# Two trunk layers on one core: a quarter of layer 1's modulation columns moved to TensorE in the fifth k phase

## The chip, the cores and the metric

The kernel runs on one core of a Trainium2 chip. The metric is device time in microseconds, median of several executions. Before the change it is 1356.29 us (three runs, 1355.13 to 1356.93).

## The reference

Two layers are applied to 384 tokens (128 context tokens and 256 latent tokens) of width 2048, all in fp32. Each layer makes three modulation vectors per group from a conditioning vector (`c_ctx` for the context tokens, `c` for the latent ones), mixes the tokens, and adds the gated result:

```python
m = silu(cond) @ w_mod + b_mod            # w_mod: 2048 x 6144; shift, scale, gate of 2048 columns each
h = rmsnorm(x) * (1 + scale) + shift
y = x + gate * mixer(h @ w_in) @ w_out
```

Layer 0's mixer is a gated linear recurrence (HGRN2) beside grouped attention; layer 1's is windowed attention with a sink. Layer 1's shift and scale columns, 4096 of them, are needed only when layer 0 is done, since layer 1's `h` is made from layer 0's output.

## The kernel before

All engines' work is laid down by one Python program; a framework then schedules it: it goes by the order of the program, prefers what is marked high priority, and lets an instruction that it takes to be ready pass one that it takes to be not ready. On the chip each engine works its list strictly in that order.

**Products.** A weight piece of 128x1024 fp32 numbers is loaded (`w_piece`, L365), split on ScalarE into a rounded part `whi` and on VectorE into a rest `wlo`, and multiplied on TensorE with the tokens' two parts `hh` and `hl`, three products for each pair. So each weight number costs one load, one ScalarE cast, one VectorE subtraction and three matmuls. Most pieces belong to a `group` of 512 output columns (L375); their raw tiles are the four buffers of the tag `raw`.

**The start.** Layer 0's input can't be modulated until layer 0's shift and scale columns are known, so the first six groups of columns of `l0_w_in` are made in five phases of k tiles, `START = ((0, 1), (1, 3), (3, 6), (6, 10), (10, 16))` (L38): all six groups take the k tiles of a phase (`start_group`, L720, with raw tiles of their own, tag `sraw`, three buffers), and meanwhile TensorE makes the modulation columns of the next phase's k tiles (`start_mod`, L740). For that a `w_mod` block is the moving operand and the 32-column tile `cs32` of conditioning numbers the stationary one, so a matmul uses 32 of the array's 128 columns; k tiles 0, 1, 2, 3 modulo 4 go to four different strips of 32 (L751). A `start_mod` step loads one 512 KB block into a `raw` buffer and issues the matmuls of its k tiles: four of 256 columns in the usual form, eight of 128 in the other. fp32 matmuls stand in the trace as two records each. At the end of a pair the sums are copied out (`ev`), transposed, added up over the strips (`ms`), and biases are added (`mod_cols`, L249).

**Layer 1's modulation and all gates** are made on VectorE in the background. `mod_part(l, k0)` (L291) makes 1024 columns: 16 loads of 512 KB into `mraw` (three buffers, L271), for each of them two multiply-adds of 128x1024 into `acc`, then four matmuls with a matrix of ones, a copy, four transposes and `mod_cols`. The parts are a list, `mods` (L776): four parts for layer 1 (shift and scale columns), then the first gates of layer 0 (`mod_gates`, L311). `pump` (L348) is called after each piece of products. It may run a unit (one load and two multiply-adds) when two budgets allow it: `pace[1]` units per call, and a planner's clock, by which VectorE's planned work may not run ahead of TensorE's. Both clocks are added up from the program's own cost formulas (L56 to L66). In the start the pace is `RATE0 = 0.6` (L777), in the later groups 2.0.

The loop of the phases (L780) spreads the next phase's `start_mod` steps evenly over the steps of products; in the fifth phase there is nothing left to spread, and only products and `mods` units run:

```python
        for j, _ in enumerate(start_products(k0, k1)):
            while done < (j + 1) * n_nxt // n:
                next(nxt, None)
                done += 1
            pump()
```

After the fifth phase come the other groups of layer 0 (the first ones, 512 columns as moving operand, use the `raw` buffers again), the recurrence and the attention as queued side work, the output projection, and layer 1.

Of the kernel before, what the change touches and what calls it, by code (L numbers as in the profile page):

```python
# [7 lines left out]
F32 = mybir.dt.float32  # L8
# [3 lines left out]
ALU = mybir.AluOpType  # L12
AX = mybir.AxisListType

P = 128
D = 2048
KT = D // P
# [5 lines left out]
RATE0 = 0.6  # L23
RAWB = 4
HIB = 3
LOB = 2
T2B = 2
# [18 lines left out]
def trunk_kernel(ctx: ExitStack, tc: tile.TileContext, I, O):  # L46
# [39 lines left out]
    nc = Core()  # L86
# [3 lines left out]
    wpool = ctx.enter_context(tc.tile_pool(name="wpool", bufs=1))  # L90
    hpool = ctx.enter_context(tc.tile_pool(name="hpool", bufs=1))
    tpool = ctx.enter_context(tc.tile_pool(name="tpool", bufs=1))
    mpool = ctx.enter_context(tc.tile_pool(name="mpool", bufs=1))

    st_ctx = ctx.enter_context(ExitStack())
    spool = st_ctx.enter_context(tc.tile_pool(name="spool", bufs=1))
# [5 lines left out]
    def nm(s):  # L102
        uid[0] += 1
        return f"{s}_{uid[0]}"

    def px():
        return psx.tile([P, 512], F32, tag="px", name=nm("px"))

    def t6(tag, dt=F32):
        return tpool.tile([P, 1536], dt, tag=f"t{tag}", name=nm(f"t{tag}"))  # L110
# [6 lines left out]
    queue, due, pace = [], [], [0.0, 0.0]  # L117
# [24 lines left out]
    ident = ct[:, C_ID:C_ID + P]  # L142
# [39 lines left out]
    cs32 = spool.tile([P, KT * 32], F32, name="cs32").rearrange("p (k c) -> p k c", k=KT)  # L182
# [63 lines left out]
    def w_view(w, k0, nk, c0, n=512):  # L246
        return w[k0 * P:(k0 + nk) * P, c0:c0 + n].rearrange("(k p) c -> p k c", p=P)

    def mod_cols(l, k0, nk, cp):  # L249

        like = (lambda a: a.rearrange("p (h b) c -> p h b c", h=2)) if len(cp.shape) == 4 else (lambda a: a)
        nc.vector.tensor_tensor(
            out=like(modc[l][:, k0:k0 + nk, :]), in0=cp,
            in1=like(bcol[l][:, k0:k0 + nk].unsqueeze(2).broadcast_to([P, nk, 2])), op=ALU.add)
        if KT <= k0 < 2 * KT:
            q = slice(k0 - KT, k0 - KT + nk)
            nc.vector.scalar_tensor_tensor(
                out=acol[l][:, q, :], in0=modc[l][:, k0:k0 + nk, :], scalar=1.0,
                in1=gcol[l][:, q].unsqueeze(2).broadcast_to([P, nk, 2]), op0=ALU.add, op1=ALU.mult)
# [31 lines left out]
    def mod_part(l, k0):  # L291

        acc = yield from mod_acc(l, k0 * P)
        ps = px()
        for j in range(4):
            nc.tensor.matmul(ps[32 * j:32 * j + 32, :], lhsT=ones[:, 0:32],
                             rhs=acc[:, j % 2, 512 * (j // 2):512 * (j // 2) + 512], start=True, stop=True)
        ev = mpool.tile([P, 512], F32, tag="t2", bufs=T2B, name=nm("ev"))
        with tc.high_priority(BOOST):
            nc.scalar.copy(ev, ps)  # L300
        for _ in range(EVY):
            yield
        cp = px()
        for b in range(4):
            nc.tensor.transpose(cp[:, b * P:b * P + P], ev[:, b * P:b * P + P], ident)
        mod_cols(l, k0, 8, cp.rearrange("p (b h c r) -> p h b c r", b=4, h=2, c=2)[:, :, :, :, 0])
        yield
# [3 lines left out]
    def mod_gates(l, g0, tags, ready):  # L311

        acc = yield from mod_acc(l, 2 * D + 512 * g0)
        while not ready[0]:
            yield
        for i in range(2):
            c0 = 2 * D + 512 * (g0 + i)
            gb = t6(tags[i])[:, 0:1024].rearrange("p (c n) -> p c n", c=2)
            for c in range(2):
                nc.gpsimd.dma_start(gb[:, c], I[f"l{l}_b_mod"][c0:c0 + 512].partition_broadcast(P))  # L320
            for c in range(2):
                ps = px()
                a = acc[:, c, 512 * i:512 * i + 512]
                hi = mpool.tile([P, 512], F32R, tag="t2", bufs=T2B, name=nm("ahi"))
                nc.scalar.copy(hi, a)
                lo = mpool.tile([P, 512], F32R, tag="t2", bufs=T2B, name=nm("alo"))
                nc.vector.tensor_tensor(out=lo, in0=a, in1=hi.bitcast(F32), op=ALU.subtract)
                nc.tensor.matmul(ps, lhsT=ones_r, rhs=hi, start=True, stop=False)
                nc.tensor.matmul(ps, lhsT=ones_r, rhs=lo, start=False, stop=True)
                nc.vector.tensor_tensor(out=gb[:, c], in0=ps, in1=gb[:, c], op=ALU.add)  # L330
            gates[l, g0 + i] = gb
        yield
# [3 lines left out]
    mods, rows, now = [], [], []  # L336
# [123 lines left out]
    def modulate(l, q, xt, rb, hq=None, parts=((0, 4),)):  # L460

        hh, hl = hq_tiles(q) if hq is None else hq
        for k0, k1 in parts:
            x = xt[:, k0:k1]
            nc.vector.tensor_tensor(out=x, in0=x, in1=rb.unsqueeze(1).broadcast_to([P, k1 - k0, T]), op=ALU.mult)
            for k in range(k0, k1):
                for c, s in CT:
                    kt = 4 * q + k
                    nc.scalar.activation(xt[:, k, s], xt[:, k, s], AF.Identity, bias=modc[l][:, kt, c:c + 1],  # L469
                                         scale=acol[l][:, kt, c:c + 1])  # L470
            nc.scalar.copy(hh[:, k0:k1], x)  # L471
            nc.vector.tensor_tensor(out=hl[:, k0:k1], in0=x, in1=hh[:, k0:k1].bitcast(F32), op=ALU.subtract)
        return hh, hl
# [238 lines left out]
    def pairs(k0, k1):  # L712

        out = []
        while k0 < k1:
            out.append((k0, min(2, k1 - k0, 4 - k0 % 4)))
            k0 += out[-1][1]
        return out
# [21 lines left out]
    def start_mod(k0, k1):  # L740

        for k, nk in pairs(k0, k1):
            n, k8 = nk * P, 8 // nk
            ps = px()
            for part in range(2):
                for i in range(2 * nk):
                    raw = wpool.tile([P, k8, n], F32, tag="raw", bufs=RAWB, name=nm("mraw"))
                    nc.sync.dma_start(raw, w_view(I["l0_w_mod"], k8 * i, k8, D * (1 - part) + k * P, n))
                    for j in range(k8):
                        kt = k8 * i + j  # L750
                        nc.tensor.matmul(ps[32 * (j % 4):32 * (j % 4) + 32, part * n:part * n + n],  # L751
                                         lhsT=cs32[:, kt, :], rhs=raw[:, j], start=(kt < 4), stop=(kt >= KT - 4))
                    if part == 0 or i < 2 * nk - 1:
                        yield
            ev = mpool.tile([P, 512], F32, tag="t2", bufs=T2B, name=nm("ev"))
            nc.scalar.copy(ev[:, 0:2 * n], ps[:, 0:2 * n])
            cp = px()
            for b in range(2 * nk):
                nc.tensor.transpose(cp[:, b * P:b * P + P], ev[:, b * P:b * P + P], ident)

            sums = spool.tile([P, 8], F32, tag="ms", bufs=2, name=nm("ms"))[:, 0:4 * nk].rearrange("p (b c) -> p b c", c=2)
            nc.vector.tensor_reduce(
                out=sums, in_=cp[:, 0:2 * n].rearrange("p (b j r) -> p b r j", j=4, r=32)[:, :, 0:2, :], axis=AX.X,
                op=ALU.add)
            for part in range(2):
                mod_cols(0, KT * (1 - part) + k, nk, sums[:, nk * part:nk * part + nk, :])
            modulate(0, k // 4, xT[k // 4], rb0, h0[k // 4], ((k % 4, k % 4 + nk),))
            yield

    def start_products(k0, k1):  # L770
        for acc, c0 in first:
            yield from start_group(acc, c0, k0, k1, k0 == 0)

    phases = START
    ready0 = [False]
    mods += [mod_part(1, k0) for k0 in (16, 24, 0, 8)] + [mod_gates(0, 0, "KL", ready0)]  # L776
    pace[1] = RATE0  # L777
    for _ in start_mod(*phases[0]):
        pass
    for i, (k0, k1) in enumerate(phases):  # L780
        nxt, n_nxt = iter(()), 0
        if i + 1 < len(phases):
            k2, k3 = phases[i + 1]
            nxt, n_nxt = start_mod(k2, k3), 4 * (k3 - k2)
        n = len(first) * len(pairs(k0, k1))
        done = 0
        for j, _ in enumerate(start_products(k0, k1)):
# [4 lines that stand above are left out]
        for _ in nxt:  # L792
            pass
        if i == 1:
            load_params()
# [200 lines left out]
    for g in range(2):  # L996
        later(3, lambda g=g: norm_oA(g))
        ps = group_b(W0, 4096 + 512 * g, h0)
# [71 lines left out]
    for i, (c0, n) in enumerate(COLS):  # L1070
# [4 lines left out]
        ps = group_b(I["l0_w_out"], c0, o0, n, (6,) if last else ())  # L1075
# [101 lines left out]
    for c0, n in COLS:  # L1177
# [4 lines left out]
        ps = group_b(I["l1_w_out"], c0, o1, n)  # L1182
# [4 lines left out]
        for b in range(3):  # L1187
            for h in range(0, n, half):
# [3 lines left out]
                                        op=ALU.mult)  # L1192
# [60 lines left out]
```

## Time and profile before

| | |
|---|---|
| median of three runs | 1356.29 us |
| the profiled execution | 1356.77 us, of which 1355.0 us span |
| TensorE busy | 1321.0 us (97%) |
| VectorE busy | 1019.0 us (75%) |
| ScalarE busy | 647.9 us (48%) |
| DMA | 265.42 MB, mean 196 GB/s |
| mean granted TensorE clock | 0.993 |

A matmul's duration in the profile is longer than the distance to the next one, because matmuls are pipelined; what a matmul or a block of them takes from the engine is read from start to start. `mm` are the product accumulators, `px` all other TensorE results; `mraw` is a block of `w_mod` and `raw` one of the other weights. In names such as `mm<-hh,whi` the moving operand comes first. Nearly all TensorE and VectorE operations carry line 77, that of a helper which counts their cost, so they are told apart by their tiles.

### The profile page before, as it was taken

How to read it: one execution, taken by the hardware profiler on the slowest of the kernel's cores; microseconds unless marked ns; L12 is line 12 of the kernel's file. 1: busy time of each engine (PE TensorE's matmuls, PEld its weight loads, DVE VectorE, ACT ScalarE, POOL GpSimd, SP SyncE). 2: the span in 40 equal slices, each digit the busy share in tenths (PEclk: the TensorE clock that was granted, in tenths of full speed). 3: DMA queues.
4: the chain of work that ended last, by engine and by line, in shares of the span. 5: the costliest groups of instructions: out<-in, count | busy, mean ns of one | idle time of the engine just before them, and what ended most of it. 6: DMA issues, size and time to landing. Idle time of an engine off the chain costs nothing.

```text
span 1355.0 us, 19101 instructions
## 1 busy us (share of the span) xinstructions
PE 1321.0 (97%) x7093; PEld 1125.7 (83%) x7093; DVE 1019.0 (75%) x1602; ACT 647.9 (48%) x1297; POOL 72.4 (5%) x84
## 2 busy tenths in 40 slices
PE   5899999999999999999999999999999999999998
PEld 4678888997888878787987887888888999998887
DVE  5678757998998745896998969995656664499743
ACT  4532233476655534755433347345766763352221
POOL 1000000000000021101000000200000101000000
PEclk8899999999999999999999999999999999999999
DMA  9989989755555334576778854784332345457642
GB/s 284 304 289 331 317 289 319 236 160 179 176 174 181 97 106 138 167 232 201 242 244 254 297 184 133 234 283 119 92 94 81 104 118 166 129 181 254 210 152 84
DMA packets 138317, 265.42 MB, mean 196 GB/s; under 512 B 8944, under 2 KB 46768, under 8 KB 138224
## 3 DMA queue, kind: packets, MB, share of 16 engines
q1 hardware_dynamic: 132592, 246.52, 56.9%
q0 software_dynamic: 5376, 17.60, 4.5%
q8 instruction: 56, 0.92, 0.3%
q14 instruction: 37, 0.30, 0.1%
q10 hardware_dynamic: 256, 0.08, 0.0%
HBM read 256.04 MB, written 8.13 MB: 195 GB/s over the span
## 4 chain that ended last, share of the span: by engine, by line
PE 91%; DMA 4%; DVE 3%; ACT 1%; POOL 1%; issue 0%; DVEq 0%; ACTq 0%; SPq 0%; POOLq 0%
PE mm L77 77%; PE px L77 14%; DMA raw<-in_l_w_in_dram 2%; DMA mraw<-in_l_w_mod_dram 1%; DVE wlo L77 1%; DVE acc L77 1%; DMA tB<-in_x_sample_dram 0%; ACT whi L370 0%; POOL sm L444 0%; DVE tB L77 0%; DMA rowc<-in_c_dram 0%; DVE tG L77 0%; ACT tE L469 0%; DVE tH L77 0%; POOL r L444 0%
## 5 line engine op out<-in xcount | busy, mean ns | idle before, releaser
L370 ACT CAST whi<-raw 128x1024 fp32r<-128x1024 f32 (+1 forms) x270 | 278.4, 1032 | 500.1 <-PE mm L77 393.7
L77 DVE TENSOR_TENSOR wlo<-raw,whi 128x1024 fp32r<-128x1024 f32 (+1 forms) x270 | 323.4, 1198 | 188.0 <-PE mm L77 148.6
L77 PE MATMUL mm<-whi,hh 128*128 128x512 f32 x1008 | 398.9, 396 | 0.0
L77 PE MATMUL mm<-wlo,hh 128*128 128x512 f32 x1008 | 391.7, 391 | 3.2 <-DVE wlo L77 3.2
L77 PE MATMUL mm<-whi,hl 128*128 128x512 f32 x1008 | 393.5, 391 | 0.6 <-DVE hl L77 0.6
L77 DVE SCALAR_TENSOR_TENSOR acc<-mraw,csil,acc 128x1024 f32<-128x1024 f32 x240 | 299.0, 1279 | 9.0 <-DMA mraw<-in_l_w_mod_dram 9.0
L77 PE MATMUL mm<-hh,whi 128*128 128x384 f32 x768 | 264.4, 347 | 7.1 <-ACT hh L471 4.6
L77 PE MATMUL mm<-hl,whi 128*128 128x384 f32 x768 | 259.2, 338 | 0.0
L77 PE MATMUL mm<-hh,wlo 128*128 128x384 f32 x768 | 254.5, 338 | 0.2 <-DVE wlo L77 0.2
L77 PEld LDWEIGHTS mm<-wlo,hh 128*128 128x128 f32 x1008 | 189.3, 188 | 42.7 <-DVE wlo L77 5.8
L77 PEld LDWEIGHTS mm<-whi,hl 128*128 128x128 f32 x1008 | 189.3, 188 | 40.8 <-DVE hl L77 1.5
L77 PEld LDWEIGHTS mm<-whi,hh 128*128 128x128 f32 x1008 | 189.4, 188 | 39.3 <-ACT tE L824 0.8
L77 PEld LDWEIGHTS mm<-hh,whi 128*128 128x128 f32 x768 | 145.3, 190 | 22.2 <-issue 10.1
L77 PEld LDWEIGHTS mm<-hh,wlo 128*128 128x128 f32 x768 | 144.8, 189 | 2.7 <-DVE wlo L77 1.0
L77 PEld LDWEIGHTS mm<-hl,whi 128*128 128x128 f32 x768 | 145.5, 190 | 1.2 <-issue 0.2
L623 ACT ACTIVATE p<-px,nb,rs 128x384 f32<-128x384 f32 (+1 forms) x72 | 42.4, 596 | 15.0 <-DVE nb L77 14.5
L77 PE MATMUL px<-mraw,cs 128*32 128x256 f32 (+1 forms) x576 | 40.4, 377 | 4.9 <-DMA mraw<-in_l_w_mod_dram 4.9
L633 ACT ACTIVATE p<-p,sum 128x384 f32<-128x384 f32 (+1 forms) x72 | 36.1, 540 | 15.1 <-DVE sum L77 13.2
L77 DVE TENSOR_REDUCE mx<-px 128x1 f32<-128x384 f32 (+1 forms) x54 | 29.7, 567 | 9.3 <-PE px L77 8.9
L77 PEld LDWEIGHTS px<-mraw,cs 128*32 128x32 f32 x576 | 16.3, 114 | 20.0 <-issue 8.2
L77 PEld LDWEIGHTS px<-ct,p 128*128 128x128 f32 x168 | 20.1, 141 | 8.3 <-issue 2.8
L444 POOL TENSOR_TENSOR rs<-rs,nhalf 128x12 f32<-128x12 f32 x6 | 14.7, 2450 | 227.5 <-DVE rs L77 227.5
(415 smaller groups left out, 1228.5 us busy)
## 6 DMA issues: line engine op xcount, KB each, us to landing
raw<-in_l_w_in_dram SPq DMA_DIRECT2D x194, 512.0 KB, 3.9
mraw<-in_l_w_mod_dram SPq DMA_DIRECT2D x192, 512.0 KB, 5.0
raw<-in_l_w_out_dram SPq DMA_DIRECT2D x64, 512.0 KB, 4.9
raw<-in_l_w_in_dram SPq DMA_DIRECT2D x12, 256.0 KB, 6.6
tK<-in_l_b_mod_dram POOLq DMA_DIRECT2D x6, 256.0 KB, 6.0
y1d<-tA POOLq DMA_DIRECT2D x2, 768.0 KB, 5.2
tD<-y1d POOLq DMA_DIRECT2D x2, 768.0 KB, 6.0
tL<-y1d POOLq DMA_DIRECT2D x2, 768.0 KB, 6.2
```

The lines of the kernel that those rows point to most:

```text
L77: return f(*a, **k)
L370: nc.scalar.copy(hi, raw)
L444: nc.gpsimd.tensor_tensor(out=out, in0=out, in1=nhalf[:, 0:out.shape[1]], op=ALU.pow)
L623: nc.scalar.activation(p[:, j], ss[j], AF.Exp, bias=nb[:, j:j + 1], scale=rs[:, i + j:i + j + 1], accum_out=sm[:, j:j + 1])
L633: nc.scalar.activation(p[:, j], p[:, j], AF.Copy, scale=sm[:, j:j + 1])
```

## The change

`mods` has three parts of layer 1 instead of four: the one that begins with k0 = 8 (columns 1024 to 2047, half of the shift) is taken out. A new generator, `late_mod(1, 8)`, makes these columns on TensorE: two halves of 512 columns, each in eight steps of one 512 KB load (two k tiles of 512 columns) into a `raw` buffer and two matmuls of 512 columns, on two of the four strips, then a copy, four transposes, a reduction and `mod_cols`. Its 16 steps are spread over the 18 steps of the fifth phase. The pace of the background units is 0 in the first phase, so that they begin with the second.

```diff
+    def late_mod(l, k0):
+        for k in (k0, k0 + 4):
+            ps = px()
+            for i in range(8):
+                raw = wpool.tile([P, 2, 512], F32, tag="raw", bufs=RAWB, name=nm("mraw"))
+                nc.sync.dma_start(raw, w_view(I[f"l{l}_w_mod"], 2 * i, 2, k * P))
+                for kt in (2 * i, 2 * i + 1):
+                    nc.tensor.matmul(ps[32 * (kt % 4):32 * (kt % 4) + 32, :],
+                                     lhsT=cs32[:, kt, :], rhs=raw[:, kt % 2], start=(kt < 4), stop=(kt >= KT - 4))
+                yield
+            ev = mpool.tile([P, 512], F32, tag="t2", bufs=T2B, name=nm("ev"))
+            nc.scalar.copy(ev, ps)
+            cp = px()
+            for b in range(4):
+                nc.tensor.transpose(cp[:, b * P:b * P + P], ev[:, b * P:b * P + P], ident)
+            sums = spool.tile([P, 8], F32, tag="ms", bufs=2, name=nm("ms")).rearrange("p (b c) -> p b c", c=2)
+            nc.vector.tensor_reduce(
+                out=sums, in_=cp.rearrange("p (b j r) -> p b r j", j=4, r=32)[:, :, 0:2, :], axis=AX.X, op=ALU.add)
+            mod_cols(l, k, 4, sums)
...
-    mods += [mod_part(1, k0) for k0 in (16, 24, 0, 8)] + [mod_gates(0, 0, "KL", ready0)]
-    pace[1] = RATE0
+    mods += [mod_part(1, k0) for k0 in (16, 24, 0)] + [mod_gates(0, 0, "KL", ready0)]
     for _ in start_mod(*phases[0]):
         pass
     for i, (k0, k1) in enumerate(phases):
+        pace[1] = RATE0 if i else 0.0
         nxt, n_nxt = iter(()), 0
         if i + 1 < len(phases):
             k2, k3 = phases[i + 1]
             nxt, n_nxt = start_mod(k2, k3), 4 * (k3 - k2)
+        else:
+            nxt, n_nxt = late_mod(1, 8), 16
```

## Rows read from the trace of the kernel before

**Rows 1.** Page, part 1: busy time of the engines.

```profile
PE 1321.0 (97%) x7093; PEld 1125.7 (83%) x7093; DVE 1019.0 (75%) x1602; ACT 647.9 (48%) x1297; POOL 72.4 (5%) x84
```

**Rows 2.** Busy time by stretch: before second phase, fifth phase, attention and first output columns.

```profile
24.39:58.00 33.61, 22.87 (x173) 16.48 (x173) 19.61 (x31) 19.30 (x41) 0.00 (x0) 0.88 0.99 321
...
214.80:288.00 73.20, 73.20 (x422) 73.20 (x423) 69.82 (x72) 41.53 (x49) 1.43 (x2) 1.00 0.72 237
...
553.00:720.00 167.00, 166.25 (x848) 140.41 (x841) 151.14 (x197) 84.75 (x173) 11.87 (x17) 1.00 0.72 222
```

**Rows 3.** Waits of the whole run: who, for whom, us in total, times, longest.

```profile
DVE wlo L77 <- PE mm L77: 148.6, 67, 6.3
...
PE px L77 <- DMA mraw<-in_l_w_mod_dram: 4.9, 3, 2.8
PE mm L77 <- ACT hh L471: 4.6, 1, 4.6
PE mm L77 <- DVE wlo L77: 3.5, 4, 1.5
```

**Rows 4.** Groups of TensorE instructions in the fifth phase (214.8 to 288 us).

```profile
L77 PE MATMUL mm<-hh,whi 128*128 128x384 f32 x141 | 47.2, 335 | 1.0 <-ACT whi L370 1.0
```

**Rows 5.** TensorE in order of time, a mod_part's matmuls with ones: start, us, what.

```profile
322.03 0.39 PE L77 MATMUL mm<-wlo,hh 128*128 128x512 f32 x1
322.25 0.39 PE L77 MATMUL mm<-whi,hl 128*128 128x512 f32 x1
322.57 1.07 PE L77 MATMUL px<-acc,ct 128*32 128x512 f32 x8
323.57 0.50 PE L77 MATMUL mm<-whi,hh 128*128 128x512 f32 x1
323.90 0.39 PE L77 MATMUL mm<-wlo,hh 128*128 128x512 f32 x1
```

**Rows 6.** TensorE in order of time, start_mod blocks of one and of four matmuls.

```profile
40.53 0.34 PE L77 MATMUL mm<-hl,whi 128*128 128x384 f32 x1
40.80 0.62 PE L77 MATMUL px<-mraw,cs 128*32 128x256 f32 x2
41.34 0.98 PE L77 MATMUL mm<-hh,wlo 128*128 128x384 f32 x4
...
109.41 0.34 PE L77 MATMUL mm<-hh,wlo 128*128 128x384 f32 x1
109.68 0.64 PE L77 MATMUL px<-mraw,cs 128*32 128x256 f32 x8
110.25 0.45 PE L77 MATMUL mm<-hh,whi 128*128 128x384 f32 x1
```

**Rows 7.** TensorE in order of time, end of the part that is removed.

```profile
635.15 1.06 PE L77 MATMUL px<-acc,ct 128*32 128x512 f32 x8
636.92 0.66 PE L77 MATMUL px<-ct,ev 128*128 128x128 f32 x4 [0.71 <-ACT ev L300]
637.41 1.02 PE L77 MATMUL px<-tC,tE 128*128 128x512 f32 x2
```

**Rows 8.** Page, part 5: VectorE's multiply-adds of the modulation, whole run.

```profile
L77 DVE SCALAR_TENSOR_TENSOR acc<-mraw,csil,acc 128x1024 f32<-128x1024 f32 x240 | 299.0, 1279 | 9.0 <-DMA mraw<-in_l_w_mod_dram 9.0
```

**Rows 9.** VectorE and TensorE in order of time, just before the second phase.

```profile
52.42 0.19 DVE L77 TENSOR_REDUCE ms<-px 128x8 f32<-128x32 f32 x1 [4.68 <-PE px L77]
52.53 1.27 DVE L77 SCALAR_TENSOR_TENSOR acc<-mraw,csil,acc 128x1024 f32<-128x1024 f32 x1
53.72 0.23 DVE L77 TENSOR_TENSOR modc<-ms,par 128x4 f32<-128x4 f32 x2
...
55.00 0.16 DVE L77 SCALAR_TENSOR_TENSOR acol<-modc,par 128x4 f32<-128x4 f32 x1
...
57.97 1.33 PE L77 MATMUL mm<-hh,whi 128*128 128x384 f32 x3 [4.58 <-ACT hh L471]
```

**Rows 10.** Busy time and granted clock at the beginning of the second phase.

```profile
56.91:63.74 6.83, 5.77 (x18) 5.77 (x19) 4.31 (x5) 2.98 (x4) 0.00 (x0) 0.50 1.09 352
```

## The prediction

> **What bounds the kernel now.** I began with the page's busy times: TensorE is busy 97% of the span, VectorE 75% [rows 1]. A busy share over the whole run hides stages, so next came the busy time by stretch. The reader is to see three different places there [rows 2]. Just before the second phase of the start (24.4 to 58 us) TensorE is busy 22.9 of 33.6 us, the 16 DMA engines are busy all the time, and the granted clock is 0.88. In the fifth phase (214.8 to 288 us), where the new work goes, TensorE is busy all 73.2 us and VectorE 69.8. Where the removed part runs today (553 to 720 us) both are nearly full, 166.3 and 151.1 of 167. Two full engines don't tell which one sets the pace; the waits do. VectorE's `wlo` waited 148.6 us for TensorE, while TensorE's products waited 3.5 us for `wlo` in the whole run [rows 3]. So TensorE sets the pace, also where VectorE looks full.
>
> For the fifth phase I then took its TensorE groups. Its 18 steps have 24 products each, 432 in all; in 73.2 us that is 0.169 us per product. The only wait in the groups is 1.0 us at the phase's start [rows 4]. So whatever is put between these products makes the phase longer by what it takes.
>
> **The price of the new matmuls.** The trace of before has no block of two 32-column matmuls of 512 columns, so I bound it by its neighbours. The nearest row is the block of a `mod_part`: four matmuls of 512 columns, one for each strip, as eight records [rows 5]. The product ahead of it starts at 322.25, the second product behind it at 323.90: 1.65 us for two products and the block. Undisturbed products of this form start 0.225 us apart (322.03 to 322.25), so the block takes 1.65 - 0.45 = 1.20 us.
>
> Is a block of two cheaper than a block of four? At half the size the trace answers it [rows 6]. A single matmul of 256 columns (two records) stands between products that start at 40.53 and 41.34, 0.81 us; a block of four (eight records) between 109.41 and 110.25, 0.84 us. What a block takes does not depend on how many of the four strips it uses: the strips work side by side, and one matmul alone leaves three empty. A block of two of 512 columns thus takes what a block of four does, 1.20 us. A `late_mod` step issues exactly two, for strips 0 and 1 or 2 and 3, and yields; one step of 24 products, over 4 us of work, comes before the next. So I count 16 blocks x 1.20 = **19.2 us**.
>
> Bounds: if every step were cut in two by a product between its matmuls (as the one-matmul block of [rows 6] shows to happen), 32 x 1.20 = 38.4; if neighbouring steps were always joined, so that all four strips run, 8 x 1.20 = 9.6. The program's order is the nearest to what [rows 6] show of `start_mod`, so I take 19.2.
>
> A rule to weigh against this: the Trainium skill, "TensorEngine Tiling (Array Packing)", section Theoretical Speedup, gives up to 4 times for a small dimension of at most 32. By it, 32 matmuls on a quarter of the array each would be paid as eight full blocks, so this term would be 9.6 us and not 19.2. The rows agree that four strips together cost what one does, and for that very reason the factor is not had by a program that offers two strips at a time.
>
> **The rest, part by part.**
> - Two copies and two sets of four transposes: a set takes 637.41 - 636.92 = 0.49 us [rows 7]. Two sets: **+1.0**. The copies, reductions and additions are on ScalarE and VectorE, behind which the casts run ahead of TensorE by three `whi` and two `wlo` buffers; if that cover is gone, a late `ev` shows as an idle such as the 0.71 us in [rows 7], at most twice, 1.4 us.
> - Removed with the part: its ones block, its transposes and the 0.71 us idle between them, 635.15 to 637.41 = 2.26 us plus 0.1 us of the switch ahead of it: **-2.4** [rows 7].
> - Removed on VectorE: 32 operations of 1.28 us, 41 us [rows 8]. By [rows 3] this is hidden under TensorE, so I count 0. The next modulation in the list, layer 0's first gates, moves up into the place of the part, and VectorE gets slack later.
> - The first phase without background units. TensorE's idle of 4.58 us there ends a chain that VectorE delays: `ms` is done at 52.6, a multiply-add of 1.27 us comes in between, and `modc` starts at 53.72 [rows 9]. Without it the chain is 1.2 us shorter. The idle is followed by a stretch of 6.83 us at half the clock (0.50, that is 1.2 GHz) with 5.77 us of work [rows 10], which is 2.9 us lost. A gap of 3.4 us instead of 4.58 may or may not let the clock fall again. Bounds: nothing at the one end; at the other the whole idle and the clock, 4.58 + 2.9 = 7.5. I take the 1.2 and about a quarter of the clock's part: **-2.0**. The 2.8 us wait for `mraw` of [rows 3] is for a load issued ahead of the first background load, so I leave it.
> - Moved: the first phase's background loads and multiply-adds (0.6 units x 6 calls, 3.6 units of 2.56 us) come later by 9 us of VectorE work, in phases that then hold one part less. Covered, 0.
> - SP's queue: 16 loads of 512 KB are added in the fifth phase, and the removed part's 16 go from its place. A late load waits for a `raw` buffer, so for TensorE's step four before it; behind it in SP's queue stand the product pieces (three buffers ahead), the `mraw` loads, and the next group's first four weight pieces, which today have the `raw` buffers at once and then only from the thirteenth late step on. That is three steps, over 12 us, ahead of their use. The phase's traffic becomes (237 GB/s x 73.2 us + 8.4 MB) / 93 us = 277 GB/s, below the 321 that [rows 2] show sustained. I count 0; without this cover a piece or two would be late, some 2 to 4 us.
> - POOL's queue: only the recurrence's first state load, which waits for the start's memory to be given back, comes some 20 us later, together with all that uses it. 0.
>
> Sum: 19.2 + 1.0 - 2.4 - 2.0 = **+15.8 us**. The profiled execution took 1356.77 us (span 1355.0 and 1.8 around it), 0.5 us over the median of the runs; added to it, 1372.6, and against the median **1372 us**.
>
> **The rivals.**
> 1. *The steps are joined.* The scheduler may put two neighbouring steps side by side, because loads come in pairs or since it takes a step's data to be late; then four strips work and 8 blocks cost 9.6 us. This is also the time that the speedup rule would give. For it: blocks in `start_mod` do get moved. Against it: 24 products lie between two steps. Time: 1372 - 9.6 = 1362 us. Chance 0.13.
> 2. *VectorE is the real bound of the middle* (ends on the other side). If from 553 to 720 us VectorE's 151 us of work set the pace, taking out 41 us [rows 8] would give back up to 41 and the kernel would be at 1372 - 41 = 1331; it is faster than before as soon as about 16 us more than the 2.4 counted come back there. Against it: `wlo` waits for TensorE and not the other way round [rows 3], and TensorE is busy 166.25 of 167 us [rows 2]; less than 1 us is idle there. Chance 0.06, somewhere from 1340 to 1352.
> 3. *The start gives back much more*: the whole idle and the clock of [rows 9, 10], and the waits for `mraw` of [rows 3]: 7.5 + 4.9 instead of 2.0, so 1372 - 10.4 = 1362. Chance 0.06. Only together with rival 1 would it come near to no change, 1352.
> 4. *Cut blocks and late pieces*: a third of the steps cut in two (5 x 1.2 = 6) and a wait for a piece or two (3): 1381. Chance 0.10.
>
> My forecast itself has 0.65.
>
> **How the numbers follow.** About 0.2%, 2.7 us, is what a measurement of this kernel can tell from no change. Faster by more needs rival 2, or rivals 1 and 3 together: 0.07. Within it: rival 1 with a good part of rival 3: 0.06. Slower: 0.87. The range that holds 8 in 10 goes from rival 1's 1362, less 2 for the start's unknown, to half of rival 4's excess: 1360 to 1378.
>
> **What the profile after would show.** Right: in the fifth phase 16 blocks `px<-mraw` of 128x512, four records each, alone between products, each with 1.2 us from product to product beyond its neighbours; that phase some 93 us long instead of 73; TensorE's idle unchanged there; three ones blocks instead of four; VectorE's busy time about 40 us less and the span not shorter for it; no `acc` between `ms` and `modc` ahead of the second phase. Wrong: blocks of eight records (rival 1), a stretch between 553 and 720 us that is shorter by ten or more (rival 2), no half clock after the first phase and no idle there (rival 3), `whi` casts waiting for loads at the end of the fifth phase (rival 4).

## The result and the profile after

The changed kernel takes **1368.84 us** (median of four runs, 1368.73 to 1368.92) against 1356.61 us for the kernel before in the runs beside it: ratio 1.0086, 95% interval 1.0066 to 1.0106. The forecast was 1372, the range 1360 to 1378. The profiled execution has a span of 1367.2 us, 12.2 more than before, so the profiles carry the whole difference.

The page's busy times after, to be read against [rows 1]:

```profile
PE 1339.5 (98%) x7153; PEld 1128.0 (83%) x7153; DVE 983.8 (72%) x1573; ACT 647.2 (47%) x1298; POOL 73.8 (5%) x84
```

TensorE has 18.5 us more, VectorE 35.2 us less, and the time follows TensorE. The busy time by stretch (columns as in [rows 2]): the first phase, the half-clock stretch behind it, the fifth phase, and the stretch in which the part was removed.

```profile
22.83:53.84 31.01, 22.94 (x188) 17.52 (x188) 11.79 (x23) 19.88 (x41) 0.00 (x0) 0.83 0.90 281
54.53:57.94 3.41, 3.41 (x24) 2.63 (x23) 1.44 (x3) 0.37 (x1) 0.00 (x0) 0.50 1.03 380
210.21:306.58 96.37, 96.37 (x520) 78.36 (x516) 76.45 (x87) 42.48 (x50) 0.00 (x0) 1.00 0.81 274
564.00:733.00 169.00, 168.93 (x850) 142.43 (x850) 137.09 (x179) 86.79 (x163) 9.92 (x17) 1.00 0.64 202
```

In the fifth phase TensorE is busy all 96.37 us, with no idle at all, and VectorE's share falls from 95% [rows 2] to 79%. The stretch at half the clock is 3.41 us long instead of 6.83 [rows 10]; that is not steady, for in the executions of e3 and e6 (below), whose first phase is the same, it is 6.83 us again. In the last stretch VectorE is down to 81% from 91%, and TensorE is as full as it was. The waits of the run say the same (as in [rows 3]):

```profile
DVE wlo L77 <- PE mm L77: 175.4, 81, 5.1
...
PE px L77 <- DMA mraw<-in_l_w_mod_dram: 7.7, 5, 3.1
...
PE mm L77 <- DVE wlo L77: 1.4, 2, 0.8
```

VectorE waits longer for TensorE than before, 175.4 instead of 148.6 us, and TensorE less for `wlo`, 1.4 instead of 3.5.

**Where the time goes** is read by the products: both kernels make 5328 of them, so the n-th of one is set against the n-th of the other (start times from the two traces).

| product | before | after | difference |
|---|---|---|---|
| 73rd, start of the second phase | 57.97 | 53.84 | -4.1 |
| 217th, start of the third phase | 92.38 | 86.17 | -6.2 |
| 721st, start of the fifth phase | 214.79 | 210.21 | -4.6 |
| 1153rd, end of the fifth phase | 289.80 | 306.58 | +16.8 |
| 2737th, output projection | 723.09 | 738.38 | +15.3 |
| 2881st | 760.2 | 772.4 | +12.2 |
| last | 1349.93 | 1362.00 | +12.1 |

The start gains, the fifth phase loses 21.4 us, and 4.7 come back later. One row corrects this table. Before, the ones block of the first part stood in the fourth phase; after, it stands in the fifth, interleaved with the first late step. TensorE in order of time before, with the two idles at the beginning of the fifth phase:

```profile
194.88 1.04 PE L77 MATMUL px<-acc,ct 128*32 128x512 f32 x8
...
213.16 0.66 PE L77 MATMUL px<-ct,ev 128*128 128x128 f32 x4 [0.71 <-ACT ev L756]
214.79 0.44 PE L77 MATMUL mm<-hh,whi 128*128 128x384 f32 x1 [0.98 <-ACT whi L370]
```

TensorE in order of time after, the first late step and one of the others:

```profile
219.19 0.62 PE L77 MATMUL px<-mraw,cs 128*32 128x512 f32 x2
219.21 0.62 PE L77 MATMUL px<-acc,ct 128*32 128x512 f32 x2
219.64 0.60 PE L77 MATMUL px<-mraw,cs 128*32 128x512 f32 x2
219.67 1.43 PE L77 MATMUL px<-acc,ct 128*32 128x512 f32 x6
...
230.71 0.33 PE L77 MATMUL mm<-hl,whi 128*128 128x384 f32 x1
230.88 0.34 PE L77 MATMUL mm<-hh,wlo 128*128 128x384 f32 x1
231.15 1.05 PE L77 MATMUL px<-mraw,cs 128*32 128x512 f32 x4
232.13 0.45 PE L77 MATMUL mm<-hh,whi 128*128 128x384 f32 x1
232.42 0.34 PE L77 MATMUL mm<-hl,whi 128*128 128x384 f32 x1
```

So part of the -4.6 at the 721st product is work put off, not saved. At the 1153rd both kernels have done the same work but for the late matmuls. The lower rows show a late block as most stand there: four records (two matmuls) alone between products. From 230.71 to 232.42 are three products and the block; three products take 3 x 0.173, so the block takes 1.19 us, and so do the twelve others that stand alone. Sixteen at this price are 19.0 us, and the first set of late transposes takes about 0.45. The start therefore gave 19.5 - 16.8 = 2.7 us net. Of this 1.7 are the two idles of the upper fence, 0.71 and 0.98, which are gone after. Another 0.35 come from the first late step: it and the ones block, interleaved, take 2.04 us together and not 1.20 + 1.19. Only about 0.6 is left of the 6.2 us. As far as the trace shows, the rest is lost in the third and fourth phase, where the products cut the `start_mod` matmuls into 13 and 17 blocks instead of 11 and 13, at about 0.35 us for each switch more, and where TensorE has small idles of 0.2 to 0.7 us.

Before the second phase the chain of [rows 9] has no multiply-add in it any more (VectorE and TensorE in order of time, after):

```profile
49.64 0.19 DVE L77 TENSOR_REDUCE ms<-px 128x8 f32<-128x32 f32 x1 [3.96 <-PE px L77]
49.87 0.23 DVE L77 TENSOR_TENSOR modc<-ms,par 128x4 f32<-128x4 f32 x2
50.06 0.17 DVE L77 SCALAR_TENSOR_TENSOR acol<-modc,par 128x4 f32<-128x4 f32 x1
...
53.84 1.12 PE L77 MATMUL mm<-hh,whi 128*128 128x384 f32 x4 [0.70 <-ACT hh L471]
```

From `ms` to `modc` it is 0.23 us instead of 1.30.

### The profile page after: what moved, and what is told of

Read it like the earlier page. It is cut to its first block, busy times and chain, and to the rows that moved or that the text cites. A ratio compares the mean times of both kernels' runs of the same rounds, so it can differ in the third digit from the quotient of the medians.

```text
span 1367.2 us, 19203 instructions
## 1 busy us (share of the span) xinstructions
PE 1339.5 (98%) x7153; PEld 1128.0 (83%) x7153; DVE 983.8 (72%) x1573; ACT 647.2 (47%) x1298; POOL 73.8 (5%) x84
## 4 chain that ended last, share of the span: by engine, by line
PE 93%; DVE 2%; DMA 2%; ACT 1%; issue 1%; SPq 0%; POOL 0%; DVEq 0%; ACTq 0%; POOLq 0%
PE mm L77 78%; PE px L77 15%; DMA mraw<-in_l_w_mod_dram 1%; DVE wlo L77 1%; DVE acc L77 0%; DMA tA<-in_x_sample_dram 0%; DMA raw<-in_l_w_in_dram 0%; DMA tab<-in_l_b_qnorm_dram 0%; ACT whi L370 0%; DVE tG L77 0%; DVE tH L77 0%; DVE tB L77 0%; POOL r L444 0%; DVE tab L77 0%; ACT tF L469 0%
## 5 line engine op out<-in xcount | busy, mean ns | idle before, releaser
L77 DVE TENSOR_TENSOR wlo<-raw,whi 128x1024 fp32r<-128x1024 f32 (+1 forms) x270 | 323.2, 1197 | 232.5 <-PE mm L77 175.4
L77 DVE SCALAR_TENSOR_TENSOR acc<-mraw,csil,acc 128x1024 f32<-128x1024 f32 x210 | 261.7, 1276 | 3.7 <-DMA mraw<-in_l_w_mod_dram 3.5
L77 PEld LDWEIGHTS mm<-hh,whi 128*128 128x128 f32 x768 | 144.5, 189 | 28.3 <-issue 12.2
L77 PE MATMUL px<-mraw,cs 128*32 128x256 f32 (+2 forms) x640 | 58.4, 396 | 7.8 <-DMA mraw<-in_l_w_mod_dram 7.7
L77 PE MATMUL px<-ct,p 128*128 128x128 f32 x168 | 24.8, 274 | 0.0
```

What stands on the lines that cost most here:

```text
L77: return f(*a, **k)
```

## Experiments

Two theories stood against each other. The first: TensorE sets the pace, a late block costs its 1.2 us wherever it lies, and VectorE's work is cover. The second: VectorE or the start's order holds the time, and the late matmuls only uncover it. A ratio below is against the kernel before in runs on the same chip. One execution may stand 2 to 3 us off its median (the kernel before ran from 1353.3 to 1360.5 us over all of them), so differences of one or two us between two traces tell where something happened and not exactly how much.

**e2_late_only: the change without its pace.**

```diff
-        pace[1] = RATE0 if i else 0.0
+        pace[1] = RATE0
```

> The changed kernel with the old pace in the first phase, so that only the move of the part to TensorE is left. My theory: the start is that of before (second phase from 58 us, fifth phase from about 214.8), the fifth phase costs its 22 us, the later stages give back about 5: 1373 us. Rival: the start's 4.6 us came with the shorter list: 1369 us.

Measured: 1369.72 us, ratio 1.0096 [1.0078, 1.0114]. The start's new pace is thus worth 0.9 us by the medians, 1.3 by the spans, although the second phase begins later here: at the 145th product it is 5.6 us behind the changed kernel, at the 721st only 1.4. The time is nearer the rival's 1369 us than the 1373, but not for the rival's reason, since the second phase begins at 57.63 us, as before. At the 1153rd product e2 is 18.1 us behind the kernel before, 1.4 less than its late work of 19.5; 0.9 of these stand already at the 433rd product, ahead of any late step. Of the two idles at the fifth phase's beginning, 1.69 us in all, 0.98 are left (TensorE in order of time):

```profile
211.63 0.45 PE L77 MATMUL mm<-hh,whi 128*128 128x384 f32 x1 [0.34 <-ACT whi L370]
...
212.89 0.44 PE L77 MATMUL mm<-hh,wlo 128*128 128x384 f32 x1 [0.64 <-DVE wlo L77]
```

So late steps alone do not remove them; e4 and e9 come back to this.

**e1_pace_only: the kernel before with the new pace, all four parts on VectorE.**

```diff
-    pace[1] = RATE0
...
+        pace[1] = RATE0 if i else 0.0
```

> The kernel before with one line of the change: the background units' pace is 0 in the first phase; all four parts of layer 1 stay on VectorE, nothing is added to the fifth phase. My theory: the changed kernel entered its fifth phase 4.6 us earlier than before (first product at 210.2 instead of 214.8 us), and that comes from this line alone, so this kernel gains 3 to 5 us, about 1352 us, and its second phase begins near 54 us instead of 58. Rival: the gain at the start needs the shorter list of parts as well, or is lost again because the four parts now begin later: 1356 to 1358 us.

Measured: 1371.16 us, 1.0106 [1.0087, 1.0126]: slower, a miss by 19 us. At the 145th product it is 6.7 us ahead of the kernel before, at the 721st 2.4, at the 2593rd 0.8 behind; by the 2737th it has lost 12 more. VectorE, TensorE and ScalarE in order of time there:

```profile
711.38 6.06 DVE L77 SCALAR_TENSOR_TENSOR acc<-mraw,csil,acc 128x1024 f32<-128x1024 f32 x5
...
712.78 0.39 PE L77 MATMUL mm<-whi,hh 128*128 128x512 f32 x1
...
719.27 0.62 ACT L325 CAST ahi<-acc 128x512 fp32r<-128x512 f32 x1 [8.54 <-DVE acc L77]
...
719.94 0.80 PE L77 MATMUL px<-ahi,ones_r 128*128 128x512 f32 x1 [6.78 <-ACT ahi L325]
```

The busy time and granted clock (columns as in [rows 2]) from there on:

```profile
716.70:726.90 10.20, 5.74 (x10) 3.29 (x11) 8.20 (x11) 2.48 (x4) 0.02 (x1) 0.50 0.48 157
```

The first gates' sums (`acc`, then `ahi`) come too late for the output projection. TensorE stands idle 6.78 us, and the granted clock is 0.50 for 10.2 us. In the kernel before, ScalarE and TensorE in order of time show how near the same two steps were to each other:

```profile
705.73 0.61 ACT L325 CAST ahi<-acc 128x512 fp32r<-128x512 f32 x1
...
708.65 0.40 PE L77 MATMUL px<-ahi,ones_r 128*128 128x512 f32 x1
```

`ahi` was ready at 706.3 and wanted at 708.65: 2.3 us of slack, and the new pace puts off 9 us of VectorE's work. The first gates' last multiply-add ends at 720.4 us instead of 707.1. In the changed kernel `ahi` stands at 655.88 and is used at 673.2, since the list is one part shorter. Behind the 2881st product e1 loses 3.7 us more, which this idle does not explain.

**e4_part_dropped: the change without the late matmuls.**

```diff
-            nxt, n_nxt = late_mod(1, 8), 16
+            nc.vector.memset(modc[1][:, 8:16, :], 0.0)
```

> The changed kernel without the late matmuls: the shift columns 1024 to 2047 of layer 1 are not computed at all but set to 0, everything else stays. It shows what taking a part from VectorE is worth when nothing is paid for it. My theory: TensorE sets the pace, so it is worth the start's 4.6 us, the part's own 2.4 us on TensorE and some 3 us at stalls of the output projection, about 10 us: 1347 us. Rival: VectorE's 41 us count in the middle: 1330 us or less.

Measured: 1354.61 us, 0.9984 [0.9972, 0.9996], so the 1347 us were missed too. Taking 41 us of work from VectorE and 2.4 from TensorE, with the new pace, gives 2 us by the medians and 4 by the spans. VectorE was not the bound. Of the gain expected at the start 2.1 us are left at the 721st product and none at the 1153rd; from there to the last product e4 gains 5.3. The late work is the difference to the changed kernel, 14.2 us by the medians and 16.1 by the spans, less than its own 20: for here the idles at the beginning of the fifth phase are back. SP's queue, ScalarE and TensorE in order of time:

```profile
203.39 13.59 SPq L368 DMA_DIRECT2D raw<-in_l_w_in_dram  x9
...
211.56 1.05 ACT L370 CAST whi<-raw 128x1024 fp32r<-128x1024 f32 x1 [1.78 <-DMA raw<-in_l_w_in_dram]
...
212.66 0.45 PE L77 MATMUL mm<-hh,whi 128*128 128x384 f32 x1 [1.20 <-ACT whi L370]
```

SP issues nine loads of `w_in` in a row, more than the product pieces of the phase have buffers for (three), so some are the next group's, in the `raw` buffers that stand free. The phase's first cast, at 211.56, starts when the third of the nine lands: two loads that are not for it were issued ahead of its own. In the kernel before it is the third load, too. In the changed kernel late loads have those buffers, SP issues the loads of `w_in` one or two at a time, the first of them is the first cast's, and the casts at 206.34 and 207.67 are done before the phase's first product at 210.21. That the late loads bring about this order, and that the order is enough, is not shown: e2 has late loads and the order, but its first load takes 9.1 us to land (issued at 201.34), and it keeps 0.98 us of idle; e9 has no late loads, yet its first cast has the first load and TensorE no idle there. The 2 us that are left of the 20 I can't place.

**e3_joined: two late steps in one, so that all four strips run.** Eight steps of two loads and four matmuls.

```diff
-            for i in range(8):
...
+            for i in range(0, 8, 2):
...
-            nxt, n_nxt = late_mod(1, 8), 16
+            nxt, n_nxt = late_mod(1, 8), 8
```

> The changed kernel, but a late step loads two blocks of 512 KB and issues four matmuls of 512 columns, one on each of the four strips; eight steps instead of sixteen, the same loads and matmuls in all. My theory: a block's price does not depend on how many strips it uses, so eight blocks of 1.2 us take the place of sixteen: 9.6 us less, 1359 us. Rival: the price is in the matmuls' columns and not in the blocks (all 32 matmuls still run): at most the eight switches between forms are saved, 8 x 0.35 = 2.8 us, so 1366 us.

Measured: 1362.24 us, 1.0038 [1.0026, 1.005]. TensorE in order of time around a block:

```profile
234.12 0.34 PE L77 MATMUL mm<-hh,wlo 128*128 128x384 f32 x1
234.39 1.06 PE L77 MATMUL px<-mraw,cs 128*32 128x512 f32 x8
235.38 0.45 PE L77 MATMUL mm<-hh,whi 128*128 128x384 f32 x1
235.66 0.34 PE L77 MATMUL mm<-hl,whi 128*128 128x384 f32 x1
```

The waits from 285 to 335 us (columns as in [rows 3]):

```profile
ACT whi L370 <- DMA raw<-in_l_w_in_dram: 9.1, 1, 9.1
...
PE mm L77 <- DVE wlo L77: 2.1, 2, 1.2
```

Four matmuls on four strips take 1.54 - 2 x 0.17 = 1.20 us, the same as two on two. By the 1153rd product 9.3 us are saved against the changed kernel. Then 2.6 are lost in the next group: its first `whi` waits 9.1 us for a load, since two late loads at a time hold `raw` buffers until the phase's end, and TensorE waits 2.1 us for `wlo`. These put the time above the theory's 1359 us.

**e5_four_strips: 16 steps as in the change, but each load holds four k tiles of 256 columns**, so that a step of 512 KB uses all four strips.

```diff
-                raw = wpool.tile([P, 2, 512], F32, tag="raw", bufs=RAWB, name=nm("mraw"))
...
+                raw = wpool.tile([P, 4, 256], F32, tag="raw", bufs=RAWB, name=nm("mraw"))
...
+                for kt in range(k4, k4 + 4):
```

> The changed kernel, but a late step loads 512 KB as four k tiles of 256 columns and issues four matmuls of 256 columns, one on each strip: still sixteen steps, one load each, the same columns in all. My theory: a block costs its switch and the columns of one strip, so a block falls from 1.19 to the 0.77 us of the start's own blocks: 16 x 0.42 = 6.7 us less in the fifth phase, 1362 us, and no wait for weights at the phase's end since the buffers come free as in the changed kernel. Rival: blocks cost by their number or by their loads, not by strips: no change, 1369 us.

Measured: 1360.91 us, 1.0031 [1.0018, 1.0043]. TensorE in order of time:

```profile
239.93 0.34 PE L77 MATMUL mm<-hh,wlo 128*128 128x384 f32 x1
240.20 0.64 PE L77 MATMUL px<-mraw,cs 128*32 128x256 f32 x8
240.77 0.45 PE L77 MATMUL mm<-hh,whi 128*128 128x384 f32 x1
241.05 0.34 PE L77 MATMUL mm<-hl,whi 128*128 128x384 f32 x1
```

A block takes 1.12 - 0.34 = 0.78 us, 0.42 less than the change's for the same 512 KB. Sixteen blocks give 6.7, and 6.7 us are gone at the last product. The loads stay as they were, and nothing is lost behind the phase.

**e6_joined_early: e3's steps, all of them within the first 14 of the 18 product steps.**

```diff
-        done = 0
+        done, m = 0, n if i + 1 < len(phases) else n - 4
...
-            while done < (j + 1) * n_nxt // n:
+            while done < min((j + 1) * n_nxt // m, n_nxt):
```

> The kernel of e3_joined with its eight steps spread over the first 14 of the 18 steps of products, so that the raw buffers come free earlier. My theory: e3 saved 9.3 us in the fifth phase and lost 2.6 us of it at the next group's first pieces, whose loads waited for these buffers; with the buffers free four steps earlier the two idles of TensorE for wlo in that group (1.21 and 0.86 us) are gone: 2 to 2.6 us less, 1360 us. Rival: the waits come from VectorE's or SP's order at that point and stay: 1362 us.

Measured: 1360.08 us, 1.0021 [1.0011, 1.0031]. Both idles that e3 has behind the phase are gone, so they did come from late loads that held the buffers at its end.

**e10_joined_four: e6 with four loads and eight matmuls in a step.**

```diff
-            for i in range(0, 8, 2):
+            for i in range(0, 8, 4):
...
-            nxt, n_nxt = late_mod(1, 8), 8
+            nxt, n_nxt = late_mod(1, 8), 4
```

> The kernel of e6_joined_early with four loads and eight matmuls of 512 columns to a step, so four blocks in all, two per strip each. My theory: a block costs a switch of 0.35 us and the columns of one strip, here 2 x 0.85, so four blocks cost 4 x 2.05 = 8.2 us where eight cost 9.6: 1.4 us less than e6, 1358 to 1359 us, near the kernel before but not below it. Rival: all four raw buffers are taken at once, a block waits for the last of its four loads and TensorE idles ahead of it: 1361 us or more.

Measured: 1358.23 us, 1.0008 [0.9998, 1.0017]. TensorE in order of time:

```profile
226.58 0.34 PE L77 MATMUL mm<-hh,wlo 128*128 128x384 f32 x1
226.85 1.92 PE L77 MATMUL px<-mraw,cs 128*32 128x512 f32 x16
228.71 0.44 PE L77 MATMUL mm<-hh,whi 128*128 128x384 f32 x1
228.99 0.34 PE L77 MATMUL mm<-hl,whi 128*128 128x384 f32 x1
```

A block of twice the columns takes 2.41 - 0.34 = 2.07 us, near the 2.05 expected, and not 2.40. With e5's 0.78 for 256 columns a strip and 1.20 for 512 this is one line: about 0.35 us for the switch to 32-column matmuls and back, and 0.42 for each 256 columns of one strip, with two strips as with four.

**e9_pace_675, e7_pace_rate, e8_rate_only: can a higher rate win back what e1 lost?** e9 and e7 are e1 with RATE0 at 0.675 and 0.75; e8 is the kernel before with 0.75 in every phase, the first too.

```diff
-RATE0 = 0.6
+RATE0 = 0.675
```

> The kernel of e1_pace_only with a pace of 0.675 units per call in phases two to five, so that the start holds as many background units as the kernel before (32.4) and none of them in the first phase. My theory: e1 lost 12 us since the list was 3.6 units late at the output projection, e7 (3.6 units ahead) lost 10 us since its extra units and the end of a part fell on the recurrence's preparation; with the list where before had it neither stall comes, and what is left of the start's gain shows: 1353 to 1357 us. Rival: any move of the units makes a new stall somewhere, because the schedule has little slack at several places: 1362 us or more.

> The kernel of e1_pace_only (four parts on VectorE, no units in the first phase) with a pace of 0.75 units per call instead of 0.6 in the other four phases: 36 units in the start instead of 28.8, 32.4 in the kernel before. My theory: e1 lost some 12 us because layer 0's first gates, last in the list, came out too late for the first columns of the output projection; with the list ahead of before's the 6.8 us idle there and the half clock behind it are gone, and a little of the start's gain stays: 1352 to 1355 us. Rival: the pace limit was not what held the list back (VectorE's budget or the later stages did): the stall stays, 1366 us or more.

> The kernel before with a pace of 0.75 instead of 0.6 in all five phases, nothing else. My theory: the first phase is that of before, the gates come earlier still, so the stall of 1.5 us at 733 us that a late load of the second gates made is gone: 1353 to 1356 us, and the difference to e7_pace_rate is what the empty first phase is worth by itself, 0 to 3 us. Rival: more units in the start delay its casts and the kernel is slower, 1358 us or more.

Measured: e9 1356.27 us, 1.0001 [0.9991, 1.0011]; e7 1364.50, 1.005 [1.0039, 1.0062]; e8 1387.86, 1.0223 [1.021, 1.0236]. e9 does what was expected: the gates are in time again, the 6.78 us idle is gone, and e1's 14 us with it; of the start's gain nothing shows in the time. Its fifth phase begins without an idle of TensorE, though it has no late loads:

```profile
211.12 0.44 PE L77 MATMUL mm<-hh,whi 128*128 128x384 f32 x1
```

e7 and e8 missed. The waits of TensorE in e7, from 280 to 340 us:

```profile
PE px L77 <- ACT ev L300: 4.3, 1, 4.3
```

The waits of TensorE in e8, whole run:

```profile
PE mm L77 <- ACT whi L370: 8.6, 2, 7.4
PE mm L77 <- DVE tL L77: 6.4, 2, 5.2
PE mm L77 <- DVE wlo L77: 6.1, 8, 3.1
PE px L77 <- ACT ev L300: 5.1, 1, 5.1
```

Against the 3.5 us that TensorE waited for `wlo` in the kernel before [rows 3], e8 has four kinds of wait, 5 to 9 us each, for work of VectorE and ScalarE, and e7 one of 4.3 us for the copy `ev` of a part, by which work that was to help has become what TensorE waits for. The rate has an upper edge in the start and a lower one at the gates; 0.6 with work in the first phase and 0.675 without lie between them. Which of the later waits each follows from the higher rate, step by step, was not tried.

## Why the prediction was right, and where it was off

**The bound was read rightly.** TensorE sets the pace, [rows 3]: e4 takes 41 us from VectorE and gains 2 to 4. Rival 2, 1331 to 1352 us, falls with it.

**The 16 blocks, +19.2: measured 19.0.** The claim taken from [rows 5, 6], that a block's time does not depend on the number of strips, is what e3, e5 and e10 test, and it holds in each of them. No block was joined with another late one, and only the first was cut, by a ones block of the same form, so neither bound of the term was met.

The Trainium skill, "TensorEngine Tiling (Array Packing)", section Theoretical Speedup, names up to 4 times for a small dimension of at most 32. e3's blocks agree with it as far as they go: the same 32 matmuls cost 8 x 1.20 = 9.6 us when four strips are offered together. The changed kernel offers two and pays 19.0, a factor of 2; one strip against four is seen at half the size only [rows 6]. The factor belongs to the order of the program, not to the shape alone. Rival 1 was thus right in the price of its blocks and wrong in that the scheduler would join them. That its 1362 us meet the 1362.24 of e3 is partly luck: the forecast it starts from was 3 us too high, and e3 lost 2.6 us behind the phase.

**Transposes, +1.0:** two sets of about 0.4 to 0.5 us, with no idle ahead of either.

**The removed part, -2.4: measured about -4.7 from the fifth phase's end to the last product**, less the second set of late transposes, so -5.2 is gained; e4, which lacks the late work, gains 5.3 there. 2.4 are the part itself. 1.8 more are two idles of the kernel before, 1.50 and 0.33 us for `wlo` near 734 and 739 us, which the sum had left standing. ScalarE, VectorE and TensorE in order of time in the kernel before:

```profile
728.73 1.05 ACT L370 CAST whi<-raw 128x1024 fp32r<-128x1024 f32 x1 [3.02 <-PE mm L77]
...
732.03 1.29 DVE L77 SCALAR_TENSOR_TENSOR acc<-mraw,csil,acc 128x1024 f32<-128x1024 f32 x1 [4.11 <-DMA mraw<-in_l_w_mod_dram]
...
733.23 1.22 DVE L77 TENSOR_TENSOR wlo<-raw,whi 128x1024 fp32r<-128x1024 f32 x1
...
734.50 0.50 PE L77 MATMUL mm<-wlo,hh 128*128 128x512 f32 x1 [1.50 <-DVE wlo L77]
```

`whi` is ready at 729.8, but VectorE takes its list in order, and ahead of `wlo` stands a multiply-add of the second gates that waits 4.11 us for its load. In the changed kernel the second gates run from 680 to 753 us instead of 719 to 781, and no load of theirs holds up `wlo` for TensorE. How late the first gates are does not decide it: in e9 they end at 709.3 us, later than the 707.1 of the kernel before, and these two idles are not there. About 1.0 I can't place. This term was the larger miss.

**The start, -2.0: measured -2.7, but of other parts.** The 1.2 us of the chain are there. The half clock shrank from 6.83 us to 3.41 in the profiled execution, which gives back about 1.2 of its 2.9 us and not 0.7, but in e3 and e6 it did not shrink. The second phase began 4.1 us earlier, more than forecast; the prediction did not have that of the 6.2 us reached at the 217th product all but about 0.6 is lost again. Against e2, which differs by the pace alone, the new pace is worth 0.9 to 1.3 us and not 2.0. The 1.7 at the fifth phase's beginning come under the next head, and 0.35 are the shared first block. Rival 3 forecast that a large gain stays and that the waits for `mraw` go with it; the gain did not last, and those waits grew from 4.9 us [rows 3] to 7.7.

**SP's queue, 0: measured -1.7**, a gain. The prediction saw that late loads take the `raw` buffers from the next group's pieces, and asked only whether those would be late. It missed that in the kernel before the load of the fifth phase's first cast stands third in its row and comes late; the idle of 1.0 in [rows 4] was the sign. That the late loads alone put this right is not shown (e2, e9). The phase's traffic was forecast well, 277 GB/s against 274 measured. Late pieces of the next group, rival 4's wait, do occur, but in e3 and not in the change.

**The moved units, "Covered, 0": right for the change, for a reason that was named too weakly.** The text said that the later phases hold one part less. e1 shows what this is worth: without it the same move costs 14 us. The cover was not TensorE's queue but the date at which the gates are wanted, and of that date [rows 3] show nothing.

Together: 19.0 + 0.9 - 2.7 - 5.2 = +12.0, the difference at the last product (12.1) but for rounding. The 1.7 of SP's queue are part of the 2.7. The forecast's +15.8 was 3.7 too high: 2.8 of it is the later term and 0.7 the start, where the unforeseen 1.7 and 0.35 stand against 1.4 of the 2.0 that did not last.

**Two readings of the prediction were off without touching the sum.** The 432 products of the fifth phase do not fit into 73.2 us: the window ended at 288, and the 1153rd product starts at 289.80, so the phase took 75.0 us, 0.174 us per product, and 96.4 after. And half of rival 4's excess of 9 us gives 1376.5 as the range's upper end, not 1378.

## What to carry to other kernels

Price small-tile matmuls by the block: the switch into and out of the form plus the columns of one strip, so offer all strips in one step, and make the blocks few. A wait list says what is late today; of background work that is moved, look up by how much it comes ahead of its use, and set that slack (here 2.3 us) against what is put off (9 us). And count the idles that stand at a stretch's edges and behind single late loads: here they gave 1.7 and 1.8 us that the sum did not have.

## What was not expected of the hardware

A stretch at half the clock (0.50, that is 1.2 GHz) came in or right behind TensorE's longest idles: before the second phase in both kernels, in e1 at the idle of 6.78 us, in e7 at that of 4.3 us, and in e8 at each of five idles between 2.2 and 7.4 us. In e1 it was 10.2 us long with 5.74 us of work in it. Products of 512 columns start 0.427 us apart in such stretches (e7) and 0.225 at the full clock of 2.4 GHz [rows 5], so that work would take about half as long there, and the idle cost up to some 3 us beyond itself. The idles of 0.71 and 0.98 us at 213 to 215 us in the kernel before were followed by none, the stretch from 214.8 us on having a granted clock of 1.00 [rows 2], nor was that of 1.50 us at 734. Not every such stretch follows a long idle: e1 has a further 3.41 us at half the clock from 1334.5 us on, behind idles of only 0.20, 0.67 and 0.29 us. It costs about half of its length, and so part of the 3.7 us that e1 loses at the end.
